# The remainders of weight units 6, 8, 10 and 12 made on GpSimd, in halves, in place of VectorE

## The chip, the cores and the metric

The kernel runs on one core of one Trainium2 chip. The metric is the device time of one execution in microseconds (us), the median of several runs. The engines are TensorE (PE, matrix products), VectorE (DVE), ScalarE (ACT), GpSimd (POOL), and SyncE (SP), which here only issues DMAs. Each engine works through its own list of instructions in order, and waits on semaphores for the others.

## The reference

A decoder trunk of two layers on 512 tokens of width 1024, in float32. Each layer normalises its input, multiplies it by one wide input projection, mixes tokens (layer 0: retention in chunks; layer 1: a causal convolution of 31 taps), adds a cross-attention over 256 memory tokens, gates the result, multiplies by an output projection, normalises, and adds to the residual:

```python
def reference(x, mem, ...):
    mem_kv = rmsnorm(mem, mem_norm_g) @ w_mem_kv
    mem_k, mem_v = jnp.split(mem_kv, 2, axis=-1)
    for i in range(DEPTH):                       # DEPTH = 2
        h = rmsnorm(x, norm_pre_g[i])
        branch, xq, gate = ...                   # from h @ w_in
        xa = memory_attention(xq, mem_k, mem_v)
        y = jnp.concatenate([branch, xa], axis=-1) * jax.nn.silu(gate)
        x = x + rmsnorm(y @ w_out, norm_post_g[i])
    return x
```

What matters here is the very beginning: the memory's projection into keys and values, and the first columns of layer 0's input projection.

## The kernel before

**Weights come in units.** All weight matrices are cut into units of 256 rows by 512 columns (a tile of 128 partitions x 2 x 512 float32, 512 KB), numbered in the order of use. Units 0 to 3 are the memory's keys, 4 to 7 its values, 8 to 11 the first 512 columns of layer 0's projection, 12 to 15 the next 512, and so on.

**Each float32 product is three matmuls.** A weight unit is split into a rounded part `whi` (ScalarE, line 192) and a remainder `wlo = wraw - whi` (VectorE, line 196, one instruction over 128 x 1024; or GpSimd, line 199, two instructions over 128 x 512, one for each half k of the unit). The activations are split in the same way (line 471 on ScalarE, line 475 on VectorE). `split3` (lines 302 to 304) then multiplies high by high, high by low and low by high. In this text hi9 is the rounded part of unit 9 and lo9 its remainder.

**Which engine makes a remainder** is decided by the unit's number in `conv_units`. Before the change, units 1 to 13 are VectorE's; from unit 14 to 55 GpSimd makes them in halves.

**Buffers set the order of the loads.** Three raw buffers (`wraw`) take turns: the load of unit i+3 (SP's list, line 172) waits until both parts of unit i have been made from the raw data. SP issues in order, so a load that waits holds the ones behind it. There are five buffers each of `whi` and `wlo`.

**Around units 6 to 14** the lists also hold: the sum of squares of the memory and of the two token halves of x. For each, ScalarE squares (line 484, two instructions), GpSimd adds the two results (line 485), VectorE reduces them (line 489), and TensorE adds over partitions by small matmuls (line 498); VectorE copies that out (line 500) and GpSimd makes the reciprocal root (lines 382 and 385). The second reciprocal root, of x, is needed to evacuate the first projection (line 870) and starts the table of rotary angles on VectorE (lines 390 and 804 on), which ScalarE's sine (line 840) waits for.

**Units 8 to 11 are used twice** (`proj_halves`): first for tokens 0 to 255, units 8 and 9 and then 10 and 11, and again for tokens 256 to 511. Their buffers come free only after the second use, so hi13 and hi14 wait for TensorE.

The whole order is written out by hand (a manual schedule): an instruction stands in its engine's list where the program calls it.

Of the kernel before, what the change touches and what calls it, by code (L numbers as in the profile page):

```python
# [46 lines left out]
LATE = 123  # L47
# [47 lines left out]
def trunk(ctx, tc, x, x_t, mem_t, pos, g_cols, w_mem, post_g, w0, w1, dw_w, dw_b,  # L95
# [11 lines left out]
    def nm(s):  # L107
        uid[0] += 1
        return f"{s}_{uid[0]}"
# [53 lines left out]
    def send(upto):  # L163

        for i in range(sent["dma"], min(upto, sent["conv"] + 3, nu)):
            sent["dma"] = i + 1
            if i in PRE:
                continue
            raws[i] = gp.tile([P, 2, G], F32, tag="wraw", bufs=3, name=nm("wraw"))
            src = units[i].rearrange("p (k c) -> p k c", k=2)  # L170
            for ks in (slice(0, 1), slice(1, 2)) if i == 0 else (slice(0, 2),):
                nc.sync.dma_start(out=raws[i][:, ks], in_=src[:, ks])

    def conv_units(upto):
        for i in range(sent["conv"], min(upto, nu)):
            send(i + 1)
            hi = gp.tile([P, 2, G], F32R, tag="whi", bufs=5, name=nm("whi"))
            lo = gp.tile([P, 2, G], F32R, tag="wlo", bufs=5, name=nm("wlo"))
            his[i], los[i] = hi, lo
            sent["conv"] = i + 1  # L180
            if i in PRE:
                nc.sync.dma_start(out=hi.bitcast(F32), in_=ahead[i][:, :, 1])
                nc.sync.dma_start(out=lo.bitcast(F32), in_=ahead[i][:, :, 0])
                continue
            raw = raws.pop(i)
            if i == 0:
                for k in range(2):
                    nc.scalar.copy(out=hi[:, k], in_=raw[:, k])
                    nc.vector.tensor_tensor(out=lo[:, k], in0=raw[:, k], in1=hi[:, k].bitcast(F32),
                                            op=ALU.subtract)  # L190
            else:
                nc.scalar.copy(out=hi, in_=raw)  # L192
            if i == 0:
                pass
            elif i < 14 or 56 <= i < 72 or i in (73, 74, 75) or i > LATE:
                nc.vector.tensor_tensor(out=lo, in0=raw, in1=hi.bitcast(F32), op=ALU.subtract)  # L196
            else:
                for k in range(2):
                    nc.gpsimd.tensor_tensor(out=lo[:, k], in0=raw[:, k],  # L199
                                            in1=hi[:, k].bitcast(F32), op=ALU.subtract)  # L200
# [40 lines left out]
    def prefetch():  # L241

        n = sent["use"]
        base = min(held) if held else n - 1
        conv_units(min(n + sent["ahead"], base + 5))
        send(sent["conv"] + 3)

    def next_unit(hold=False):
        i = sent["use"]
        sent["use"] += 1  # L250
        if hold:
            held.append(i)
        conv_units(i + 1)
        prefetch()
        return his.pop(i), los.pop(i)
# [263 lines left out]
    def evac_v(a, acc):  # L519
        nc.scalar.activation(out=mv[:, a, :], in_=acc, func=AF.Copy, scale=mr["c"][:, a:a + 1])  # L520

    conv = lambda upto: lambda: (conv_units(upto), send(upto + 3))
    mT = lambda kp: lambda: split_c(mt, kp, gcols[:, 0], mget)
    mT(0)()
# [973 lines left out]
```

## Time and profile before

| | us |
|---|---|
| median of 3 runs | 816.2 (816.07 to 820.01) |
| the profiled execution | 818.56 |
| its span, first to last instruction | 816.6 |
| PE busy in the span | 800.4 (98%) |
| DVE busy | 493.2 (60%) |
| ACT busy | 372.5 (46%) |
| POOL busy | 456.7 (56%) |

The span is that of one profiled execution. PE is busy nearly all the time, so what the time can lose or gain is in the few places where it stands idle, and in the chains that end in one of them. Rows give start, duration, engine, line, operation, the tiles, and in square brackets the engine's idle time before it and what ended that. An xN row is N instructions that followed each other, with their time together.

### The profile page before, as it was taken

The numbers are of one execution on the slowest core, as the hardware profiler recorded it, in microseconds if no ns is written. First come the engines' busy times: TensorE is split into PE (matmuls) and PEld (weight loads), VectorE is DVE, ScalarE is ACT, GpSimd is POOL, SyncE is SP. The second block draws the span as 40 slices with busy tenths as digits, with TensorE's granted clock in tenths as the row PEclk, the third lists the DMA queues.
The fourth block names the chain that finished last, engine by engine and source line by source line (L and its number), as shares of the span: only waits on it lengthen the run. The fifth ranks groups of instructions, "written<-read, shape, count | busy, mean of one in ns | idle before, by whom it ended". The sixth has DMA issues, their size and how long they took to land.

```text
span 816.6 us, 10729 instructions
## 1 busy us (share of the span) xinstructions
PE 800.4 (98%) x3910; PEld 675.4 (83%) x3910; DVE 493.2 (60%) x776; ACT 372.5 (46%) x625; POOL 456.7 (56%) x407
## 2 busy tenths in 40 slices
PE   8999999999999999999999999999999989899996
PEld 8888788888888888888888988888888878778885
DVE  5789212125655732353325579999999899656723
ACT  6752467622311233453425415545368786355511
POOL 1144754368777876411133036999775898867202
PEclk9999999999999999999999999999999999989999
DMA  7732764464364274676873364334543601323422
GB/s 265 258 106 96 243 205 137 155 206 164 132 207 163 95 218 146 210 238 212 271 243 124 130 230 149 132 130 161 179 147 98 215 31 52 127 80 104 166 92 103
DMA packets 47077, 131.14 MB, mean 161 GB/s; under 512 B 5297, under 2 KB 6961, under 8 KB 46769
## 3 DMA queue, kind: packets, MB, share of 16 engines
q1 hardware_dynamic: 46448, 130.25, 47.1%
q8 instruction: 30, 0.49, 0.3%
q10 hardware_dynamic: 576, 0.21, 0.1%
q14 instruction: 23, 0.18, 0.1%
HBM read 103.18 MB, written 27.26 MB: 160 GB/s over the span
## 4 chain that ended last, share of the span: by engine, by line
PE 74%; DVE 11%; ACT 6%; issue 3%; DMA 3%; POOL 3%; POOLq 0%; SPq 0%; DVEq 0%; ACTq 0%
PE mm L302 21%; PE mm L304 21%; PE mm L303 21%; DVE acc L1184 5%; PE tp L602 2%; DMA wraw<-in_w_mem 1%; DVE cy L1393 1%; POOL wlo L199 1%; PE acc L990 1%; ACT whi L192 1%; DVE wlo L196 1%; PE tp L971 1%; PE acc L992 1%; ACT cy L1387 1%; PE tp L948 1%
## 5 line engine op out<-in xcount | busy, mean ns | idle before, releaser
L302 PE MATMUL mm<-big,whi 128*128 128x512 f32 (+1 forms) x608 | 235.3, 387 | 1.7 <-ACT big L639 1.0
L304 PE MATMUL mm<-big,wlo 128*128 128x512 f32 (+1 forms) x608 | 228.0, 375 | 1.3 <-DVE wlo L196 1.0
L199 POOL TENSOR_TENSOR wlo<-wraw,whi 128x512 fp32r<-128x512 f32 x138 | 180.0, 1328 | 86.6 <-ACT whi L192 86.5
L303 PE MATMUL mm<-big,whi 128*128 128x512 f32 (+1 forms) x608 | 227.5, 374 | 0.0
L1184 DVE SCALAR_TENSOR_TENSOR acc<-gl,taps,acc 128x512 f32<-128x512 f32 x259 | 173.2, 746 | 0.1
L304 PE MATMUL mm<-whi,big 128*128 128x512 f32 (+1 forms) x432 | 167.1, 387 | 0.2 <-POOL big L767 0.2
L302 PE MATMUL mm<-whi,big 128*128 128x512 f32 (+1 forms) x408 | 162.4, 398 | 0.0
L303 PE MATMUL mm<-wlo,big 128*128 128x512 f32 (+1 forms) x408 | 157.8, 387 | 0.3 <-DVE wlo L196 0.3
L304 PEld LDWEIGHTS mm<-big,wlo 128*128 128x128 f32 x608 | 115.0, 189 | 23.0 <-DVE wlo L196 1.4
L302 PEld LDWEIGHTS mm<-big,whi 128*128 128x128 f32 x608 | 115.1, 189 | 21.4 <-ACT big L639 1.4
L303 PEld LDWEIGHTS mm<-big,whi 128*128 128x128 f32 x608 | 115.2, 189 | 18.8 <-issue 0.5
L192 ACT CAST whi<-wraw 128x1024 fp32r<-128x1024 f32 x111 | 115.5, 1047 | 24.5 <-PE mm L304 10.4
L1140 POOL TENSOR_TENSOR part<-part,pr 128x512 f32<-128x512 f32 x79 | 101.4, 1312 | 24.9 <-ACT pr L1139 24.7
L229 POOL TENSOR_TENSOR stage<-stage 128x512 f32<-128x512 f32 x44 | 57.2, 1301 | 103.6 <-ACT stage L228 99.8
L304 PEld LDWEIGHTS mm<-whi,big 128*128 128x128 f32 x432 | 81.1, 188 | 17.5 <-POOL big L767 0.6
L303 PEld LDWEIGHTS mm<-wlo,big 128*128 128x128 f32 x408 | 76.8, 188 | 15.5 <-DVE wlo L196 0.8
L302 PEld LDWEIGHTS mm<-whi,big 128*128 128x128 f32 x408 | 76.7, 188 | 14.7 <-issue 0.2
L196 DVE TENSOR_TENSOR wlo<-wraw,whi 128x1024 fp32r<-128x1024 f32 x42 | 56.3, 1349 | 43.0 <-ACT whi L192 43.0
L228 ACT CAST stage<-stage 128x512 fp32r<-128x512 f32 x44 | 27.3, 620 | 95.6 <-DMA stage<-in_w 53.4
L1139 ACT ACTIVATE pr<-gl,taps 128x512 f32<-128x512 f32 x79 | 53.6, 719 | 7.4 <-POOL part L1140 7.4
L1111 ACT ACTIVATE gl<-mm 128x512 f32<-128x512 f32 x12 | 7.2, 599 | 47.7 <-PE mm L304 47.7
L560 DVE TENSOR_REDUCE tiny<-tp 128x2 f32<-128x512 f32 x16 | 10.7, 687 | 25.7 <-PE tp L553 25.7
(221 smaller groups left out, 906.5 us busy)
## 6 DMA issues: line engine op xcount, KB each, us to landing
wraw<-in_w SPq DMA_DIRECT2D x104, 512.0 KB, 4.2
ahead<-stage SPq DMA_DIRECT2D x44, 512.0 KB, 5.2
stage<-in_w SPq DMA_DIRECT2D x44, 256.0 KB, 5.3
whi<-ahead SPq DMA_DIRECT2D x22, 512.0 KB, 4.2
wlo<-ahead SPq DMA_DIRECT2D x22, 512.0 KB, 5.9
wraw<-in_w_mem SPq DMA_DIRECT2D x7, 512.0 KB, 5.0
big<-in_x_t SPq DMA_DIRECT2D x2, 1024.0 KB, 7.3
o<-in_x SPq DMA_DIRECT2D x1, 2048.0 KB, 9.8
```

Source lines behind the costliest of these rows:

```text
L192: nc.scalar.copy(out=hi, in_=raw)
L196: nc.vector.tensor_tensor(out=lo, in0=raw, in1=hi.bitcast(F32), op=ALU.subtract)
L199: nc.gpsimd.tensor_tensor(out=lo[:, k], in0=raw[:, k], in1=hi[:, k].bitcast(F32), op=ALU.subtract)
L228: nc.scalar.copy(out=st[:, 1].bitcast(F32R), in_=st[:, 0])
L229: nc.gpsimd.tensor_tensor(out=st[:, 0], in0=st[:, 0], in1=st[:, 1], op=ALU.subtract)
L302: nc.tensor.matmul(dst, lh, rh, start=start, stop=False)
L303: nc.tensor.matmul(dst, lh, rl, start=False, stop=False)
L304: nc.tensor.matmul(dst, ll, rh, start=False, stop=stop)
L602: nc.tensor.matmul(po[:, h * P:(h + 1) * P], mv[:, m, h * P:(h + 1) * P], pT[:, m, h, :], start=m == 0, stop=m == 1)
L1139: nc.scalar.activation(out=pr, in_=gl[:, k:k + S], func=AF.Copy, scale=tap)
L1140: nc.gpsimd.tensor_tensor(out=parts[ct], in0=parts[ct], in1=pr, op=ALU.add)
L1184: nc.vector.scalar_tensor_tensor(out=o, in0=gl[:, k:k + S], scalar=tap, in1=ac, op0=ALU.mult, op1=ALU.add)
```

## The change

One condition gets an exception: for units 6, 8, 10 and 12 the first branch no longer holds, so they fall to the last branch, which makes the remainder on GpSimd in two halves. Units 7, 9, 11 and 13 stay on VectorE.

```diff
             if i == 0:
                 pass
-            elif i < 14 or 56 <= i < 72 or i in (73, 74, 75) or i > LATE:
+            elif i < 14 and i not in (6, 8, 10, 12) or 56 <= i < 72 or i in (73, 74, 75) or i > LATE:
                 nc.vector.tensor_tensor(out=lo, in0=raw, in1=hi.bitcast(F32), op=ALU.subtract)
             else:
                 for k in range(2):
                     nc.gpsimd.tensor_tensor(out=lo[:, k], in0=raw[:, k],
                                             in1=hi[:, k].bitcast(F32), op=ALU.subtract)
```

GpSimd's list before, from the sum of the memory's squares (first row) to the first remainder that it makes, that of unit 14 (last two rows). The rows of line 485 are the sums of squares of the memory and of the two halves of x; lines 382 and 385 the memory's reciprocal root.

```order
10 L485 TENSOR_TENSOR w_26_236<-w_26_236,w_27_237 128x1024 [waits Activation_49]
11 L382 TENSOR_SCALAR tiny_341<-tiny_337 128x2 [waits DVE_49]
12 L385 TENSOR_TENSOR tiny_343<-tiny_341,nhalf 128x2 [waits Pool_49]
13 L485 TENSOR_TENSOR w_60_413<-w_60_413,w_61_414 128x1024 [waits Activation_49]
14 L485 TENSOR_TENSOR w_73_473<-w_73_473,w_74_474 128x1024 [waits Activation_49]
15 L199 TENSOR_TENSOR wlo_546<-wraw_433,whi_545 128x512 [waits DMAHW0_49,Activation_49]
16 L199 TENSOR_TENSOR wlo_546<-wraw_433,whi_545 128x512
```

The same stretch of GpSimd's list after; wlo_313, 357, 403 and 445 are lo6, lo8, lo10 and lo12.

```order
11 L199 TENSOR_TENSOR wlo_313<-wraw_228,whi_312 128x512 [waits DMAHW7_49,PE_49,Activation_49]
12 L199 TENSOR_TENSOR wlo_313<-wraw_228,whi_312 128x512
13 L382 TENSOR_SCALAR tiny_342<-tiny_338 128x2 [waits DVE_49]
14 L385 TENSOR_TENSOR tiny_344<-tiny_342,nhalf 128x2 [waits Pool_49]
15 L199 TENSOR_TENSOR wlo_357<-wraw_283,whi_356 128x512 [waits DMAHW1_49,PE_49,Activation_49]
16 L199 TENSOR_TENSOR wlo_357<-wraw_283,whi_356 128x512
17 L199 TENSOR_TENSOR wlo_403<-wraw_335,whi_402 128x512 [waits DMAHW3_49,PE_49,Activation_49]
18 L199 TENSOR_TENSOR wlo_403<-wraw_335,whi_402 128x512
19 L485 TENSOR_TENSOR w_60_416<-w_60_416,w_61_417 128x1024 [waits Activation_49]
20 L199 TENSOR_TENSOR wlo_445<-wraw_385,whi_444 128x512 [waits DMAHW6_49,PE_49,Activation_49]
21 L199 TENSOR_TENSOR wlo_445<-wraw_385,whi_444 128x512
22 L485 TENSOR_TENSOR w_73_477<-w_73_477,w_74_478 128x1024 [waits Activation_49]
```

Eight instructions are new. The pairs of units 6 to 10 stand ahead of the first sum of x's squares, the pair of unit 12 between the two.

VectorE's list after, from the reduction of the memory's squares (first row) to the remainder of unit 13 (last row); wlo_332, 382, 433 and 538 are lo7, lo9, lo11 and lo13.

```order
10 L489 TENSOR_REDUCE w_27_237<-w_26_236 128x256
11 L196 TENSOR_TENSOR wlo_332<-wraw_263,whi_331 128x1024
12 L500 COPY tiny_338<-tp_337 128x2
13 L475 SCALAR_TENSOR_TENSOR big_301<-big_204,gcols,big_300 128x256 x4
14 L196 TENSOR_TENSOR wlo_382<-wraw_317,whi_381 128x1024
15 L475 SCALAR_TENSOR_TENSOR big_303<-big_204,gcols,big_302 128x256 x4
16 L196 TENSOR_TENSOR wlo_433<-wraw_361,whi_432 128x1024
17 L475 SCALAR_TENSOR_TENSOR big_301<-big_373,gcols,big_300 128x256 x4
18 L489 TENSOR_REDUCE w_61_417<-w_60_416 128x256
19 L475 SCALAR_TENSOR_TENSOR big_303<-big_373,gcols,big_302 128x256 x2
20 L489 TENSOR_REDUCE w_74_478<-w_73_477 128x256
21 L475 SCALAR_TENSOR_TENSOR big_303<-big_373,gcols,big_302 128x256 x2
22 L196 TENSOR_TENSOR wlo_538<-wraw_407,whi_537 128x1024
```

Before, one more remainder stood ahead of lo7 (lo6), between the four instructions of line 475 (lo8), behind the first row of big_303 (lo10), and behind lo11 (lo12). The rest is in the same order.

On SP the difference of the two lists shows the loads of units 8 (wraw_283) to 11; the wait behind each load is for the unit three before it.

```order
 L172 DMA wraw_283<-in_w 128x1024 [waits DMAHW5_49,DVE_49]
-L172 DMA wraw_316<-in_w 128x1024 [waits DMAHW7_49,DMAHW2_49,DVE_49]
-L172 DMA wraw_334<-in_w 128x1024 [waits DMAHW0_49,DVE_49]
-L172 DMA wraw_359<-in_w 128x1024 [waits DMAHW1_49,DVE_49]
-L459 DMA big_371<-in_x_t 128x2048
...
+L172 DMA wraw_317<-in_w 128x1024 [waits DMAHW2_49,DMAHW7_49,Activation_49,Pool_49]
+L172 DMA wraw_335<-in_w 128x1024 [waits DMAHW0_49,DVE_49]
+L172 DMA wraw_361<-in_w 128x1024 [waits DMAHW1_49,Activation_49,Pool_49]
+L459 DMA big_373<-in_x_t 128x2048
```

The loads stand in the same order. Those of units 9 and 11 wait for GpSimd where they waited for VectorE, and the load of x's second half (big_373) stands behind the one of unit 11.

## Rows read from the trace of the kernel before

**Rows 1.** The page: busy time of each engine, share, instructions.
```profile
PE 800.4 (98%) x3910; PEld 675.4 (83%) x3910; DVE 493.2 (60%) x776; ACT 372.5 (46%) x625; POOL 456.7 (56%) x407
```

**Rows 2.** Timeline of TensorE: start, us, line, tiles, [idle before <- releaser].
```profile
27.52 0.39 PE L303 MATMUL mm<-wlo,big 128*128 128x512 f32 x1
...
39.58 0.50 PE L303 MATMUL mm<-wlo,big 128*128 128x512 f32 x1 [0.34 <-DVE wlo L196]
...
49.05 0.95 PE L498 MATMUL tp<-ones,w 128*128 128x1 f32 x8
...
83.81 0.50 PE L302 MATMUL mm<-big,whi 128*128 128x512 f32 x1 [1.01 <-ACT big L639]
```

**Rows 3.** Timeline of VectorE and GpSimd where both make remainders, and GpSimd alone.
```profile
300.59 2.53 POOL L199 TENSOR_TENSOR wlo<-wraw,whi 128x512 fp32r<-128x512 f32 x2
...
333.73 3.53 POOL L199 TENSOR_TENSOR wlo<-wraw,whi 128x512 fp32r<-128x512 f32 x2
...
334.38 1.72 DVE L196 TENSOR_TENSOR wlo<-wraw,whi 128x1024 fp32r<-128x1024 f32 x1 [2.21 <-ACT whi L192]
```

**Rows 4.** Timeline of GpSimd, 36 to 55 us.
```profile
36.05 2.39 POOL L485 TENSOR_TENSOR w<-w,w 128x1024 f32<-128x1024 f32 x1 [7.45 <-ACT w L484]
43.30 2.41 POOL L485 TENSOR_TENSOR w<-w,w 128x1024 f32<-128x1024 f32 x1 [4.86 <-ACT w L484]
50.37 2.55 POOL L199 TENSOR_TENSOR wlo<-wraw,whi 128x512 fp32r<-128x512 f32 x2 [4.66 <-ACT whi L192]
...
53.28 1.03 POOL L385 TENSOR_TENSOR tiny<-tiny,nhalf 128x4 f32<-128x4 f32 x1
```

**Rows 5.** Timeline of ScalarE, 23 to 75 us: the casts of units 6, 9, 10, 11, 12, 14 among others.
```profile
23.59 1.05 ACT L192 CAST whi<-wraw 128x1024 fp32r<-128x1024 f32 x1 [2.16 <-DMA wraw<-in_w_mem]
...
29.32 1.05 ACT L192 CAST whi<-wraw 128x1024 fp32r<-128x1024 f32 x1 [0.86 <-PE mm L303]
...
32.46 1.04 ACT L192 CAST whi<-wraw 128x1024 fp32r<-128x1024 f32 x1
...
35.87 1.04 ACT L192 CAST whi<-wraw 128x1024 fp32r<-128x1024 f32 x1
38.67 1.05 ACT L192 CAST whi<-wraw 128x1024 fp32r<-128x1024 f32 x1 [1.75 <-DMA wraw<-in_w]
...
41.23 1.99 ACT L484 ACTIVATE w<-big 128x1024 f32<-128x1024 f32 x2
...
49.25 1.05 ACT L192 CAST whi<-wraw 128x1024 fp32r<-128x1024 f32 x1 [0.30 <-PE mm L304]
...
74.20 0.42 ACT L840 ACTIVATE q<-q 128x256 f32<-128x256 f32 x1 [11.70 <-DVE q L794]
```

**Rows 6.** Timeline of VectorE, 25 to 51 us.
```profile
25.94 1.22 DVE L196 TENSOR_TENSOR wlo<-wraw,whi 128x1024 fp32r<-128x1024 f32 x1
...
36.95 2.58 DVE L196 TENSOR_TENSOR wlo<-wraw,whi 128x1024 fp32r<-128x1024 f32 x1 [2.19 <-ACT whi L192]
...
40.90 1.67 DVE L475 SCALAR_TENSOR_TENSOR big<-big,gcols,big 128x256 fp32r<-128x256 f32 x4
42.48 2.05 DVE L489 TENSOR_REDUCE w<-w 128x256 f32<-128x1024 f32 x1
...
46.32 2.01 DVE L489 TENSOR_REDUCE w<-w 128x256 f32<-128x1024 f32 x1
...
49.04 1.21 DVE L196 TENSOR_TENSOR wlo<-wraw,whi 128x1024 fp32r<-128x1024 f32 x1
```

**Rows 7.** The chain that ended last, and SP's timeline: the loads of units 9 and 12.
```profile
25.93 3.30 DMA wraw<-in_w
...
31.66 0.33 SPq L172 DMA_DIRECT2D wraw<-in_w  x1
```

**Rows 8.** Late wait of TensorE, and the stretch around it: PE busy (count), granted clock, DMA.
```profile
711.20 0.35 PE L1356 MATMUL tp<-ones,sum 128*128 128x1 f32 x2 [2.59 <-DVE sum L1348]
...
710.00:720.00 10.00, 8.80 (x33) 0.66 0.37 139
```

## The prediction, made before the changed kernel ran

> **What bounds the kernel now.** I read the page first. TensorE is busy 98% of the span [rows 1], so work that is only moved from one helper engine to another cannot show unless it ends or starts a wait of TensorE. The idle times of TensorE came next: up to 100 us they are small, and between 20 and 80 us there is a single one, 0.34 us at 39.58, ended by VectorE's lo11; the next is 1.01 us at 83.81, ended by ScalarE [rows 2]. All the moved instructions run before 45 us. So the most that a relieved VectorE can give back here is 0.34 us and perhaps a part of the 1.01; whatever the change delays in front of TensorE is lost for good, since behind it TensorE is full.
>
> Then I read the three helpers. ScalarE makes hi9 at 29.32 as soon as its load has landed, and the chain that ended last runs through it: load of unit 9 (25.93 to 29.23), hi9, ScalarE's other work, hi11 (ends 36.91), lo11 [rows 5 to 7]. So the early part is a load chain whose first link is the end of lo6. Last I looked at how VectorE and GpSimd get in each other's way. A pair of halves takes 2.53 us alone, 1.27 each; the pair at 333.73 took 3.53, and the remainder that VectorE began in its midst took 1.72 in place of 1.22 [rows 3, 6]. They did not overlap: VectorE waited for the end of the first half, ran, and the second half waited for VectorE. Likewise lo11 began at 36.95, the sum of squares on GpSimd ended at 38.44, and lo11 ended 1.09 us behind that [rows 4, 6]. So an instruction that subtracts or adds two tiles on VectorE and one on GpSimd exclude each other, and where both have work they take turns.
>
> The Trainium skill, "Perfetto Trace Analysis", section "Optimizing Scalar/DVE Operations", speaks against the change: VectorE and GpSimd share a read port, so moving operations between those two might not help. By that rule the time freed on VectorE, 4 x 1.22 us, is worth nothing, which is a sum of zero or worse; by reading the two engines as independent the change would come out as the port rival below does. The pair of 3.53 us sides with the rule.
>
> **The change part by part.** Removed: four VectorE instructions of 1.22 us [rows 6]. Added: eight GpSimd halves, 10.1 us [rows 3]. GpSimd has room for them, so the cost is not their sum but where each stands. A remainder now takes 2.53 us, or 3.53 with a turn of VectorE, in place of 1.22: it is 1.3 to 2.3 us later. Who waits for that:
>
> *Unit 6.* hi6 ends at 24.64 [rows 5]; GpSimd starts 0.07 later, as it does behind hi14 (50.30, 50.37) [rows 4, 5], so the first half runs from 24.71 to 25.98. VectorE asks for lo7 at 25.94 [rows 6], 0.04 before that. If it gets its turn (case A), the second half ends at 24.71 + 3.53 = 28.24; if GpSimd goes on first (case B), at 27.24. TensorE wants the second half at 27.52 [rows 2]: A costs 0.77 us and about 0.1 of restart, B nothing.
>
> *The load of unit 9* waits for the end of lo6, and holds the loads behind it on SP. It goes at 28.27 (A) or 27.27 (B) in place of 25.93: +2.34 or +1.34. The load's own 3.30 us [rows 7] stays; hi9 and all that ScalarE does behind it, up to hi11, move by as much, since ScalarE has practically no idle time there.
>
> *lo11.* hi10 ends at 33.50 + 2.34 = 35.84; its pair runs to 38.44; the sum of squares, itself moved to 38.39, starts then and ends at 40.83. lo11 is locked out as before and ends 1.09 later, 41.92; TensorE goes on at 41.97 in place of 39.58 [rows 2, 4, 6]. TensorE is then 2.4 us late in A (unit 6's loss is inside that), 1.4 in B. The halves of units 8 and 10 themselves arrive in time.
>
> *Unit 12 and the second sum.* Unit 12's load waits for lo9, so in A it goes at 34.0 in place of 31.66 and hi12 ends at 42.06 in place of 39.72 [rows 5, 7]. lo12 itself is not wanted for a long time; its pair is harmful as a neighbour. Before, four instructions of line 475 (0.42 each) ran undisturbed at 40.90, and the first reduction at 42.48 lay beside GpSimd's second sum [rows 4, 6]. Now the pair (from 42.13) takes turns with those four: first half to 43.40, one instruction, second half to 45.0, two instructions to 45.8. The second sum asks at 43.30 + 2.34 = 45.64, before the fourth, and takes its 2.4 us, to 48.15. Then follow the fourth (48.55), the first reduction (2.05, to 50.6), two of line 475 (51.4) and the second reduction (2.01, to 53.4). TensorE wants that in the second half of its eight small matmuls, 49.45 before [rows 2] and 51.85 now: it waits 1.5 us, and is about 3.9 late. In B by the same steps the reduction ends at 53.0, and TensorE is 3.6 late.
>
> *Unit 14 and the root.* lo13 was done when GpSimd began unit 14's pair at 50.37 [rows 4, 6]. Now hi14, tied to TensorE, ends at 52.7, and the pair shares its time with two of line 475, pushing lo13 to 57.2; the reciprocal root (53.28 to 54.31 before) ends near 58.5, +4.2 (A), or 57.7, +3.4 (B). The rotary table on VectorE starts behind it; ScalarE waits for that at 74.20 for 11.70 us [rows 5], and TensorE's wait at 83.81 hangs on ScalarE. The slip of the root therefore replaces TensorE's own slip there: the 1.01 us idle would swallow a part of TensorE's slip only if the root slipped less.
>
> Sum: +4.2 in A, +3.4 in B. Nothing behind 84 us is changed. I take +3.7, between the two and nearer to neither, as the request of lo7 and the end of the half are 0.04 us apart. The profiled execution, 818.56 (816.6 of span and 1.96 around it), would become 822.3; the median shown is 2.36 below that execution, so the forecast is 816.2 + 3.7 = 819.9 us. That is 0.45% and so just inside what a measurement of this kernel can tell from no change, 0.5% or 4.1 us.
>
> **The rivals.**
>
> *The second collision does not happen.* If the fourth instruction of line 475 asks before the second sum (0.16 us apart above), the first reduction lies beside the sum as before, the second ends near 51.3, and TensorE does not wait. Then the slip is 2.4 to 2.8 in A, 1.4 in B: 817.6 to 819.0. For it: so small a distance. Against it: both times hang on hi12, so that a late load does not change their order.
>
> *The port is no obstacle between these instructions.* Then lo6 ends at 27.24, lo11 runs beside the sum of squares and ends at 39.3, before it did, and both reductions are in time: -0.2, 816.0 us; with part of the 1.01 us at 83.81 it could be 815.3. Against it stand the 3.53 and the 2.58 us [rows 3, 6].
>
> *The loads take longer.* Units 9 and 10 now go out almost together, and unit 11 and x's second half later and closer to unit 12. If unit 9 takes 4.5 us in place of 3.3, each later step slips by 1.2 more: 821.1.
>
> *The clock falls: clearly slower.* Behind the wait of 2.59 us at 711.20, with small matmuls around it, the granted clock was 0.66 over 10 us [rows 8]: the lower level, 1.2 GHz, for some 6.8 us, at a price of 0.34 x 10 = 3.4 us. If the wait for lo11 (2.4 us less what unit 6 has taken) or the one for the reduction does the same, the time is 819.9 + 3.4 = 823.3. [...] The Trainium skill, "TensorE: Matmul & The Clock Gate", section "Part 1: The HAM clock gate", has the same direction: an idle array falls back to the lower level.
>
> **How the numbers follow.** The forecast, with its two cases from 3.4 to 4.2, has 0.5; its own range with an uncertainty of 0.8 for the turns is 818.8 to 821.2. No second collision 0.22; longer loads 0.11; the clock 0.07; no obstacle 0.10. The range for 8 in 10 leaves out the lowest of the last and the highest of the clock: 816.5 to 823.0. Slower by over 0.5% (above 820.3): a third of the forecast's share, 0.17, the longer loads and the clock, 0.18, and about 0.02 of the rest: 0.37. Faster by over 0.5%: only what no row explains, 0.03. Within: 0.60.
>
> **What would show it.** In the changed kernel's timeline: the pair of unit 6 at 3.5 us (A) or 2.5 (B), with TensorE idle near 27.6 in A alone; the load of unit 9 issued at 27.3 or 28.3; the wait for lo11 near 41 with 1 us or more; VectorE's second reduction ending near 53 and TensorE idle before the small matmuls; the root of x ending near 58. The prediction is wrong if TensorE has no wait at the second reduction, or if lo7 and lo11 run at 1.22 us beside GpSimd's work, or if the slip at 84 us is not that of the root.

## The result, and the profile after

The changed kernel takes 822.28 us (median of 15 runs, 816.88 to 825.89), the kernel before, run alternately on the same chip, 816.14 (15 runs, 815.02 to 821.32). The ratio is 1.0054 with a 95% interval of 1.0036 to 1.0072: slower by 4.4 us, 2.9 to 5.9. (The ratio weighs all runs; the two medians alone are 6.1 apart.) Forecast were 819.9, between 816.5 and 823.0: the time is in the range, near its upper end, and the change is just beyond the 0.5% that the prediction called the limit of telling it from none. The profiled execution took 823.97, with a span of 822.2, against 818.56 and 816.6 before: +5.4 in time, +5.6 in the span.

The page after, first part; its columns are those of [rows 1].

```profile
PE 802.4 (98%) x3910; PEld 676.5 (82%) x3910; DVE 494.5 (60%) x772; ACT 372.4 (45%) x625; POOL 470.4 (57%) x415
```

VectorE has four instructions fewer, GpSimd eight more, as intended. Yet VectorE is no less busy, 494.5 us against 493.2: the four remainders saved are gone again in longer instructions. The timeline of TensorE after, its rows with a wait:

```profile
28.71 0.50 PE L303 MATMUL mm<-wlo,big 128*128 128x512 f32 x1 [1.17 <-POOL wlo L199]
...
42.40 0.50 PE L303 MATMUL mm<-wlo,big 128*128 128x512 f32 x1 [1.81 <-DVE wlo L196]
...
52.88 0.58 PE L498 MATMUL tp<-ones,w 128*128 128x1 f32 x4 [0.56 <-DVE w L489]
59.23 0.50 PE L302 MATMUL mm<-big,whi 128*128 128x512 f32 x1 [0.17 <-ACT vb L870]
...
87.87 0.50 PE L302 MATMUL mm<-big,whi 128*128 128x512 f32 x1 [1.14 <-ACT big L639]
...
662.99 2.24 PE L602 MATMUL tp<-w,mv 128*128 128x128 f32 x11 [2.34 <-ACT w L596]
...
716.84 0.35 PE L1356 MATMUL tp<-ones,sum 128*128 128x1 f32 x2 [2.62 <-DVE sum L1348]
```

Where [rows 2] had one wait of 0.34 us between 20 and 80 us, there are four now: for the second half of lo6, for lo11, for the second reduction, and a small one for the first evacuation behind the root. The wait of 0.34 at 39.58 has become 1.81 at 42.40, 2.82 later; the one at 83.81 stands at 87.87, 4.06 later. The next two rows belong to the late part of the program, to which the text returns below.

GpSimd after, with its idle times:

```profile
25.09 3.57 POOL L199 TENSOR_TENSOR wlo<-wraw,whi 128x512 fp32r<-128x512 f32 x2 [6.12 <-ACT whi L192]
...
38.87 2.39 POOL L485 TENSOR_TENSOR w<-w,w 128x1024 f32<-128x1024 f32 x1
41.22 3.72 POOL L199 TENSOR_TENSOR wlo<-wraw,whi 128x512 fp32r<-128x512 f32 x2
44.90 2.58 POOL L485 TENSOR_TENSOR w<-w,w 128x1024 f32<-128x1024 f32 x1
53.15 3.91 POOL L199 TENSOR_TENSOR wlo<-wraw,whi 128x512 fp32r<-128x512 f32 x2 [5.67 <-ACT whi L192]
...
57.42 1.03 POOL L385 TENSOR_TENSOR tiny<-tiny,nhalf 128x4 f32<-128x4 f32 x1
```

These are the pair of unit 6, the first sum of x's squares, the pair of unit 12, the second sum, the pair of unit 14, and the root. VectorE after, in the same stretch:

```profile
26.31 1.23 DVE L196 TENSOR_TENSOR wlo<-wraw,whi 128x1024 fp32r<-128x1024 f32 x1 [1.87 <-ACT whi L192]
...
39.79 2.55 DVE L196 TENSOR_TENSOR wlo<-wraw,whi 128x1024 fp32r<-128x1024 f32 x1 [3.78 <-ACT whi L192]
42.27 5.88 DVE L475 SCALAR_TENSOR_TENSOR big<-big,gcols,big 128x256 fp32r<-128x256 f32 x4
48.07 1.97 DVE L489 TENSOR_REDUCE w<-w 128x256 f32<-128x1024 f32 x1
...
50.75 1.99 DVE L489 TENSOR_REDUCE w<-w 128x256 f32<-128x1024 f32 x1
...
53.44 1.21 DVE L196 TENSOR_TENSOR wlo<-wraw,whi 128x1024 fp32r<-128x1024 f32 x1
```

Read the two side by side. lo7 (26.31 to 27.54) lies inside the pair of unit 6, which takes 3.57 us where a pair alone takes 2.53 [rows 3]: VectorE had its turn between the halves. lo11 asks at 39.79, in the midst of GpSimd's sum (38.87 to 41.26), and takes 2.55: it ends 1.08 behind the sum. The four instructions of line 475, 1.67 us together before [rows 6], take 5.88 between the pair of unit 12 and the second sum, and push both reductions.

ScalarE's cast of unit 9, and the chain that ended last, after (of the chain: start, duration, engine or DMA, tile):

```profile
32.12 1.05 ACT L192 CAST whi<-wraw 128x1024 fp32r<-128x1024 f32 x1 [3.28 <-DMA wraw<-in_w]
```

```profile
25.09 3.57 POOL wlo L199 x2
28.69 3.33 DMA wraw<-in_w
```

The load of unit 9 goes when GpSimd's second half ends, 2.76 later than in [rows 7], and hi9 follows 2.80 later.

Late in the program the windows after show one thing more (busy time and count of PE, PEld, DVE, ACT, POOL, then the granted clock, DMA share, GB/s):

```profile
660.00:664.00 4.00, 1.66 (x10) 1.20 (x9) 4.00 (x8) 3.97 (x7) 3.92 (x4) 0.94 0.00 0
664.00:668.00 4.00, 4.00 (x18) 3.64 (x18) 3.00 (x6) 2.72 (x7) 3.31 (x3) 0.63 0.00 0
```

Behind the wait of 2.34 us at 662.99 the granted clock falls to 0.63 over 4 us, part of that at the lower level, 1.2 GHz. In the execution of before the row that answers reads as follows, and the clock stays at 1.00 from 656 to 672 us (second row, a window).

```profile
658.92 2.05 PE L602 MATMUL tp<-w,mv 128*128 128x128 f32 x16 [2.29 <-ACT w L596]
656.00:672.00 16.00, 13.71 (x81) 11.64 (x80) 15.30 (x25) 14.24 (x25) 14.72 (x12) 1.00 0.10 34
```

There TensorE was 662.99 - 658.92 = 4.07 late; at 716.84 it is 716.84 - 711.20 = 5.64 late [rows 8]. So of the +5.6 in the span, some 4.1 were lost before 88 us, and 1.6 between the two places, where the clock fell.

### The profile page after: what moved, and what is told of

Read it like the earlier page. It is cut to its first block, busy times and chain, and to the rows that moved or that the text cites. A ratio compares the mean times of both kernels' runs of the same rounds, so it can differ in the third digit from the quotient of the medians.

```text
span 822.2 us, 10737 instructions
## 1 busy us (share of the span) xinstructions
PE 802.4 (98%) x3910; PEld 676.5 (82%) x3910; DVE 494.5 (60%) x772; ACT 372.4 (45%) x625; POOL 470.4 (57%) x415
## 4 chain that ended last, share of the span: by engine, by line
PE 69%; DVE 13%; ACT 6%; issue 4%; POOL 3%; DMA 3%; SPq 0%; POOLq 0%; DVEq 0%; ACTq 0%
PE mm L302 19%; PE mm L304 19%; PE mm L303 19%; DVE acc L1184 5%; DMA wraw<-in_w_mem 2%; POOL wlo L199 2%; PE tp L602 1%; DVE cy L1393 1%; PE acc L990 1%; DVE cy L1262 1%; ACT whi L192 1%; PE tp L971 1%; PE acc L992 1%; ACT cy L1387 1%; PE tp L948 1%
## 5 line engine op out<-in xcount | busy, mean ns | idle before, releaser
L199 POOL TENSOR_TENSOR wlo<-wraw,whi 128x512 fp32r<-128x512 f32 x146 | 193.6, 1349 | 100.3 <-ACT whi L192 100.2
L196 DVE TENSOR_TENSOR wlo<-wraw,whi 128x1024 fp32r<-128x1024 f32 x38 | 51.4, 1361 | 47.9 <-ACT whi L192 47.9
```

The source lines that it names most:

```text
L199: nc.gpsimd.tensor_tensor(out=lo[:, k], in0=raw[:, k], in1=hi[:, k].bitcast(F32), op=ALU.subtract)
```

## The experiments

Every run is timed against the kernel before on the same chip. One caution for all of them: the load of unit 6 itself, which no edit touches, lands at another time in each profiled execution (hi6 starts at 23.59 in that of before, at 23.96 after, between 22.86 and 25.00 in all), and what hangs on it moves along. Slips are therefore counted from the start of hi6. For the changed kernel at the wait near 84 us: (87.87 - 23.96) - (83.81 - 23.59) = 3.69 us. The kernel before, profiled a second time, shows +0.33 by the same count, so smaller differences are not read. Each kernel has one profiled execution.

| run | ratio, 95% interval | slip at lo11 | wait for 2nd reduction | slip of the root's end | slip near 84 us |
|---|---|---|---|---|---|
| the changed kernel | 1.0054 (1.0036 to 1.0072) | 2.45 | 0.56 | 3.77 | 3.69 |
| only6 | 1.0053 (1.0028 to 1.0077) | 2.72 | none | 3.16 | 3.46 |
| u6_8_10 | 1.0063 (1.0035 to 1.0091) | 2.92 | none | 3.37 | 3.52 |
| u8_10_12 | 1.0011 (0.9989 to 1.0032) | 0.21 | none | 0.29 | 0.39 |
| whole6 | 1.0017 (0.9995 to 1.0040) | 1.23 | none | 1.29 | 1.60 |
| raw9_apart | 1.0026 (1.0009 to 1.0043) | 0.94 | 0.55 | 2.26 | 2.42 |
| u6_8_10_raw9 | 1.0011 (0.9992 to 1.0030) | 0.96 | none | 1.41 | 1.49 |
| whole6_raw9 | 1.0030 (1.0010 to 1.0050) | 0.77 | 0.54 | 2.12 | 2.26 |
| u8_raw9 | 1.0014 (0.9992 to 1.0035) | -0.03 | 0.56 | 1.31 | 1.41 |
| before_raw9_apart | 1.0009 (0.9992 to 1.0025) | -0.70 | none | -0.26 | -0.06 |
| after_u14_vector | 1.0052 (1.0030 to 1.0075) | 2.58 | 0.55 | 2.87 | 3.02 |
| before_u14_vector | 0.9995 (0.9976 to 1.0013) | 0.07 | none | -0.99 | 0.12 |

**Which unit: only6, u8_10_12, u6_8_10.** The condition names fewer units (the three added lines are those of the three kernels, in that order):

```diff
-            elif i < 14 and i not in (6, 8, 10, 12) or 56 <= i < 72 or i in (73, 74, 75) or i > LATE:
+            elif i < 14 and i not in (6,) or 56 <= i < 72 or i in (73, 74, 75) or i > LATE:
+            elif i < 14 and i not in (8, 10, 12) or 56 <= i < 72 or i in (73, 74, 75) or i > LATE:
+            elif i < 14 and i not in (6, 8, 10) or 56 <= i < 72 or i in (73, 74, 75) or i > LATE:
```

> Only unit 6 is moved to GpSimd; 8, 10 and 12 are back on VectorE. Load theory (the end of lo6 sets the load of unit 9 and by it hi9, hi11 and lo11): the load of unit 9 is about 2.5 us later than before, TensorE is 2.4 to 2.8 us late after lo11, does not wait for the second reduction, and is 2.7 to 3.6 us late at the wait before 88 us; most of the changed kernel's 4.06 us is there. Rival (each of the four pairs costs its own share): a quarter, 1.0 us.

> Units 8, 10 and 12 are on GpSimd, unit 6 is back on VectorE. Load theory: the load of unit 9 goes at its old time, TensorE is at most 0.3 us late after lo11; what is left is the collision of unit 12's pair with line 475 and the second sum, 0 to 1.7 us, so 0.3 to 2.0 us in all before 88 us. Rival (each pair costs its share): three quarters, 3.0 us.

> Units 6, 8 and 10 are on GpSimd, unit 12 is back on VectorE. Collision theory: TensorE is 2.8 us late after lo11 as in the changed kernel, but the wait of 0.56 us for the second reduction is gone, and before 88 us it is 2.8 to 3.6 us late. Rival (the wait for the reduction comes from the late loads alone, not from unit 12's pair): the 0.56 us stay and the slip is 4.0 us.

With unit 6 alone most of the slip is there; with the other three alone, nothing that can be measured. TensorE in only6:

```profile
28.64 0.50 PE L303 MATMUL mm<-wlo,big 128*128 128x512 f32 x1 [1.06 <-POOL wlo L199]
...
42.59 0.50 PE L303 MATMUL mm<-wlo,big 128*128 128x512 f32 x1 [2.05 <-DVE wlo L196]
...
52.02 0.95 PE L498 MATMUL tp<-ones,w 128*128 128x1 f32 x8
...
87.56 0.50 PE L302 MATMUL mm<-big,whi 128*128 128x512 f32 x1 [1.52 <-ACT big L639]
```

The wait for lo11 is there, the one for the second reduction is not. Taken by themselves these three runs seem to clear the pair of unit 12. The runs further down show that this would be the wrong reading. Part of it lies in unit 9's load, which took 3.63 us in only6's execution and 3.79 in u6_8_10's, against 3.33 in the changed kernel's, for no reason that the edits give: 0.3 and 0.5 us of their slips come from there.

**The turn inside the pair: whole6.** The changed kernel, with lo6 in one GpSimd instruction, so that VectorE finds no gap in it:

```diff
+            elif i == 6:
+                nc.gpsimd.tensor_tensor(out=lo, in0=raw, in1=hi.bitcast(F32), op=ALU.subtract)
             else:
                 for k in range(2):
```

> As the changed kernel, but the remainder of unit 6 is one GpSimd instruction over 128 x 1024, so that VectorE cannot take a turn in its midst. Turn theory: lo6 ends about 2.4 us after it starts (3.57 in the changed kernel), the load of unit 9 goes 1.1 us earlier than there, TensorE waits 0.2 us or less for unit 6, is 1.4 to 1.8 us late after lo11, and 2.9 to 3.4 us late before 88 us. Rival (the end of lo6 hangs on GpSimd's speed, not on the turn): no difference, 4.06 us.

GpSimd and VectorE in whole6:

```profile
25.47 2.39 POOL L198 TENSOR_TENSOR wlo<-wraw,whi 128x1024 fp32r<-128x1024 f32 x1 [6.07 <-ACT whi L192]
...
26.70 2.23 DVE L196 TENSOR_TENSOR wlo<-wraw,whi 128x1024 fp32r<-128x1024 f32 x1 [2.03 <-ACT whi L192]
```

Now lo7 is the one that waits (2.23 in place of 1.23), and lo6 is done 2.39 after its start in place of 3.57. The slip at lo11 falls from 2.45 to 1.23, by just the 1.2 us of VectorE's turn, and the time to 1.0017. In sizes the expectation was missed: TensorE still waits 0.57 us for unit 6 (0.2 or less expected), and near 84 us it is 1.60 late, where 2.9 to 3.4 were expected. The gain there is larger than the turn, since the collision of unit 12 costs TensorE no wait either in this kernel; why, is told below.

**The load of unit 9: raw9_apart, before_raw9_apart.** Unit 9's raw data gets a buffer of its own, so that its load need not wait for lo6; in the changed kernel, and in the kernel before. The loads behind it move up too: that of unit 10 now waits for lo6, of unit 11 for lo7, of unit 12 for lo8.

```diff
-            raws[i] = gp.tile([P, 2, G], F32, tag="wraw", bufs=3, name=nm("wraw"))
+            raws[i] = gp.tile([P, 2, G], F32, tag="w4" if i == 9 else "wraw",
+                              bufs=4 if i == 9 else 3, name=nm("wraw"))
```

> As the changed kernel, but the raw data of unit 9 has a buffer of another kind, so that its load does not wait for lo6; unit 10's load now stands behind lo6, unit 11's behind lo7. Load theory: hi9 starts near 28.5 us (32.12 in the changed kernel), TensorE still waits 0.8 to 1.2 us for unit 6's second half, but is only 0.9 to 1.3 us late at lo11 (2.82 there) and 1.0 to 2.0 us late before 88 us (4.06 there). Rival (VectorE's turns beside GpSimd's eight halves make the slip, loads or not): 3.5 us or more before 88 us.

> The kernel before, with unit 9's raw data in a buffer of its own, so that its load need not wait for lo6. If the load of unit 9 is the first link of the chain to lo11 in the kernel before too, TensorE's 0.34 us at 39.58 goes and little else changes, since the load waited only some 0.9 us there and the root of x still hangs on unit 14: ratio 0.999 to 1.000, the same within what can be measured. The rival, that the load was not on the path before: 0.34 us stay.

TensorE in raw9_apart:

```profile
28.67 0.50 PE L304 MATMUL mm<-wlo,big 128*128 128x512 f32 x1 [0.93 <-POOL wlo L200]
...
40.86 0.50 PE L304 MATMUL mm<-wlo,big 128*128 128x512 f32 x1 [0.32 <-DVE wlo L197]
...
51.34 0.58 PE L499 MATMUL tp<-ones,w 128*128 128x1 f32 x4 [0.55 <-DVE w L490]
...
86.57 0.50 PE L303 MATMUL mm<-big,whi 128*128 128x512 f32 x1 [1.39 <-ACT big L640]
```

lo6 is as late as before (the pair still takes 3.56), yet the wait for lo11 falls from 1.81 to 0.32: the loads behind lo6 were the link between the two. But near 84 us the slip is 2.42, between what was expected of the theory and of its rival: more than the late load was at work. In the kernel before, the load was a link too: lo11 comes 0.70 earlier, counted from hi6. But 0.23 us of TensorE's wait remain where none was expected, and near 84 us nothing is left of the gain.

**The second collision: whole6_raw9, u8_raw9, u6_8_10_raw9.** Combinations of the edits above: both edits in the changed kernel; the three units without unit 6, with the buffer apart; and raw9_apart with unit 12 back on VectorE.

> The changed kernel with both halves of the cause taken away: lo6 in one GpSimd instruction (so that lo7 gets no turn inside it) and unit 9's raw buffer apart. If late lo6 by VectorE's turn and the late load of unit 9 are the whole cause, TensorE loses 0.4 to 0.6 us at unit 6 and nothing more at lo11, and its slip before 88 us, counted from the cast of unit 6, is 0.3 to 0.9 us: ratio 1.000 to 1.001. If the pairs of units 8, 10 and 12 cost something of their own beside them, the slip is over 1.3 us.

> Units 8, 10 and 12 on GpSimd, unit 6 on VectorE, and unit 9's raw buffer apart: the version that could beat the kernel before, if VectorE's relief is worth something once the load of unit 9 is early. Then TensorE has no wait at 39.6 and the root of x comes earlier: ratio 0.998 to 0.9995. If the relief is worth nothing, since lo11 is locked out by GpSimd's sum of squares as before, the ratio is 1.000 to 1.002.

> The run with unit 9's raw buffer apart, once more, with the remainder of unit 12 back on VectorE. In that run TensorE's slip at the wait near 84 us, counted from the cast of unit 6, was 2.42 us: 0.94 of it at lo11, 1.48 behind it, where the pair of unit 12 stands between the instructions of line 475 and TensorE waits 0.55 us for the second reduction. If that second collision comes with the pair of unit 12, TensorE has no wait at the small matmuls of line 498, and the slip is 1.4 to 1.8 us; VectorE pays 1.2 us for lo12 itself. The rival, that the collision of line 475 with the second sum makes the same delay whether the pair stands between or not: slip 2.2 us or more. In time the two stand 0.6 to 1.0 us apart, near 1.0015 and 1.0026 as ratios.

whole6_raw9 was a miss: TensorE lost 0.18 us at unit 6 and 0.30 at lo11, and was still 2.26 late near 84 us. The first expectation of u8_raw9, that VectorE's relief would show once the load is early, failed as well: TensorE still waits 0.69 us for lo11, and 0.56 for the second reduction. Its other case, that the relief is worth nothing (1.000 to 1.002), fits the 1.0014.

```profile
39.86 0.50 PE L304 MATMUL mm<-wlo,big 128*128 128x512 f32 x1 [0.69 <-DVE wlo L197]
...
50.35 0.58 PE L499 MATMUL tp<-ones,w 128*128 128x1 f32 x4 [0.56 <-DVE w L490]
```

The table tells what is common. Between lo11 and 84 us the slip grows by 1.24 to 1.49 in the four kernels that have a wait for the second reduction as after does, with unit 12's pair among the instructions of line 475 (after 3.69 - 2.45, raw9_apart, whole6_raw9, u8_raw9). It grows by 0.05 to 0.74 in those without. after_u14_vector has that wait and that pair too, and grows by 0.44 only; it will show the way that the delay takes. u6_8_10_raw9 differs from raw9_apart in unit 12 alone, and was to decide. Its VectorE:

```profile
38.34 3.78 DVE L197 TENSOR_TENSOR wlo<-wraw,whi 128x1024 fp32r<-128x1024 f32 x2 [3.22 <-POOL wlo L200]
42.04 3.81 DVE L476 SCALAR_TENSOR_TENSOR big<-big,gcols,big 128x256 fp32r<-128x256 f32 x4
```

Line 475 (476 there) takes 3.81 with the second sum alone as its neighbour, against 5.88 with the pair as well; TensorE does not wait at the small matmuls, and the slip near 84 us is 1.49, as expected, in place of 2.42. So the pair of unit 12 costs 0.9 us there. The two times, 1.0011 and 1.0026, have intervals that overlap; it is the traces that tell them apart. They also show where the 0.9 us arise, unit 14's pair and lo13 in raw9_apart (first two rows) and in u6_8_10_raw9:

```profile
51.61 3.90 POOL L200 TENSOR_TENSOR wlo<-wraw,whi 128x512 fp32r<-128x512 f32 x2 [5.68 <-DVE big L476]
51.90 1.22 DVE L197 TENSOR_TENSOR wlo<-wraw,whi 128x1024 fp32r<-128x1024 f32 x1
...
51.79 3.03 POOL L200 TENSOR_TENSOR wlo<-wraw,whi 128x512 fp32r<-128x512 f32 x2 [6.22 <-ACT whi L193]
51.20 1.21 DVE L197 TENSOR_TENSOR wlo<-wraw,whi 128x1024 fp32r<-128x1024 f32 x1
```

Unit 14's pair starts 27.68 and 27.70 us behind hi6, at the same time. In raw9_apart VectorE is late by the collision, lo13 falls inside the pair and has its turn between the halves, as lo7 has in unit 6's; in u6_8_10_raw9 lo13 began before the pair. The pair is 0.87 us longer, and the root 2.26 - 1.41 = 0.85 later. It takes 3.90 to 3.92 us in all four kernels that grow by 1.24 or more, and 2.55 to 3.03 in the others; in after_u14_vector GpSimd does not make it. In the changed kernel, too, unit 14's pair starts 2.41 us later than before, as lo11 does (2.45), and the rest of the root's 3.77 is the pair's 3.91 in place of 2.55. So the pair of unit 12 costs its time by way of unit 14's pair and the root, and not by the wait for the second reduction.

In u8_10_12 the pair of unit 12 stands at the same place and hurts nothing:

```profile
41.22 2.73 POOL L199 TENSOR_TENSOR wlo<-wraw,whi 128x512 fp32r<-128x512 f32 x2 [1.16 <-ACT whi L192]
```

There hi12 waited for its load until 40.10, and the work of line 475 began only at 41.59, behind ScalarE's line 471. It still met the pair and took 3.43 us in place of 1.67; but the second sum came only at 44.73, with the fourth instruction of line 475 already begun, and did not lock it out. In whole6 it went the same way. ScalarE waited 1.78 us (u8_10_12) and 1.44 (whole6) for unit 12 behind hi11, and 0 to 0.88 in the five kernels that have the wait for the second reduction. So whether the collision reaches TensorE goes with how far unit 12 lands behind unit 11; no run changes this landing alone.

**What hangs on the root: after_u14_vector, before_u14_vector.** Unit 14's remainder, which stands ahead of the root in GpSimd's list, goes to VectorE, in either kernel (`i < 15` in place of `i < 14`).

> As the changed kernel, but the remainder of unit 14 is on VectorE, so that the reciprocal root of x stands behind no pair on GpSimd. Root theory (the slip at the wait before 88 us is that of the root): the root ends near 57.3 us in place of 58.45, TensorE is about 3.0 us late there in place of 4.06. Rival (TensorE's own lateness after the reductions, 3.46 us, sets it): 3.5 us or more.

> The kernel before with one edit: the remainder of unit 14 is on VectorE too. If the wait of 1.01 us at 83.81 us hangs on the root, the root ends near 53.0 us in place of 54.31, the wait goes, and the kernel is 1.0 us faster than before (0.12%, under what a comparison can tell, but to be seen in the trace). Rival (the wait hangs on ScalarE's or the loads' own pace): no change, 1.01 us stay.

In the changed kernel the slip fell by 0.67 us, from 3.69 to 3.02, as expected; the median did not show it. In the kernel before, the root came 0.99 earlier, and the wait near 84 us stayed (1.09 at 83.80): a miss. VectorE there shows why:

```profile
57.34 1.22 DVE L513 TENSOR_TENSOR mkT<-mkT,tp 128x1024 f32<-128x1024 f32 x1 [1.98 <-PE tp L396]
```

In before the same instruction stands at 57.43 with 0.96 of idle time. It waits for TensorE's small matmuls of line 396, and the rest of the rotary table is queued behind it: an earlier root makes it wait 1.0 longer, no more.

**The kernel before, once more: before_again.**

> The kernel before, profiled once more, with no edit: how much the start of hi6, lo11's wait and the waits at 84, 659 and 711 us differ between two executions of the same program. Expected: hi6 within 1.5 us of 23.59, the wait before lo11 and the one at 84 us as before to 0.2 us, and another clock at one of the late waits if these are chance.

```profile
39.70 0.50 PE L303 MATMUL mm<-wlo,big 128*128 128x512 f32 x1 [0.88 <-DVE wlo L196]
...
658.20 2.05 PE L602 MATMUL tp<-w,mv 128*128 128x128 f32 x16 [1.17 <-ACT w L596]
```

That the waits would be as before to 0.2 us was a miss: the one for lo11 was 0.88 in place of 0.34, since the load of unit 6 landed later against TensorE, the one near 84 us 1.33 in place of 1.01, and the one at 658 1.17 in place of 2.29. The same program differs by as much as some of the prediction's terms.

No version is shown to be faster than the kernel before; the lowest ratio, 0.9995 of before_u14_vector, is the same within its interval.

## Why the prediction was right, and where it was not

**That helpers could only lose** held. Nearly all loss up to 88 us is in waits of TensorE for the moved work and what it delays: its waits between 20 and 88 us add up to 4.85 us, 1.35 before. The pair of unit 6 took 3.56 to 3.59 us in six kernels, and lo6 in one piece 2.39 with a waiting lo7 of 2.23 in whole6. The Trainium skill, "SBUF — State Buffer", section "Who interferes with whom", says that an instruction of VectorE with two inputs in SBUF contends with one of GpSimd that reads it. These times agree with that.

***Unit 6*: the mechanism was right, its case was left open for no need.** Case A said 24.71 + 3.53; less the 0.37 us by which this execution's hi6 came later, 28.66 is 28.29. The pair took 3.56 to 3.59 wherever unit 6 was made in halves: VectorE's turn was no toss-up. The forecast of +3.7 lay halfway to case B, which no run showed. Case A by itself gave +4.2, 820.4 us; the slip of TensorE in the profiled execution is 4.06, or 3.69 from hi6. That 3.69 meets the 3.7 is luck: averaging with case B took off about as much as the steps of units 12 and 14, below, had added too much.

***The load of unit 9*** was right: 3.33 us against 3.30, and 1.5 us of slip at lo11 go when it no longer hangs on lo6 (raw9_apart: 0.94 for 2.45). ***lo11*** was right: TensorE at 41.97 forecast, 42.40 measured, 42.03 less the 0.37.

***Unit 12 and the second sum*: right in kind, too large in its wait.** The collision is there as described, pair, line 475 and second sum taking turns. The second reduction ends at 52.74, 52.37 less the 0.37 (53.4 forecast), and TensorE waits 0.56 in place of 1.5. The mis-sized term is unit 12's load: it went at 34.45 (34.0 forecast), but took 5.2 us where the sum kept the 6.9 of before. So hi12 was to end at 42.06, and ended at 40.84. What the step didn't see is what only6 shows: without the pair VectorE must make lo12 itself, and line 475 then meets the second sum. So part of the growth behind lo11 stays without the pair: 0.74 us in only6 and 0.60 in u6_8_10, against 1.24 in the changed kernel. The pair is thus worth some 0.5 to 0.6 us there, and 0.9 with unit 9's load out of the way; the slips of 3.52 (u6_8_10) and 3.69 (after) lie closer together only since unit 9's load was slower in u6_8_10's execution.

***Unit 14 and the root*: the number right, the reason only in part.** The root ended at 58.45, 58.08 less the 0.37, and 58.5 were forecast. Unit 14's pair shared its time with VectorE, but not as described: the two of line 475 were not held up (0.87 us at 52.66), and lo13, forecast to be pushed to 57.2, had its turn inside the pair and ended at 54.65. In the table the slip near 84 us follows that of the root within about 0.3 us in all kernels with a late one. But "TensorE's wait at 83.81 hangs on ScalarE" and so on the root is not the whole: before_u14_vector shows that line 513, tied to TensorE, holds the chain too. A later root moves the wait; an earlier one does not.

**"Nothing behind 84 us is changed" failed.** The rival of the clock looked at the waits for lo11 and the reduction, but there the clock did not fall: it is 1.00 from 28 to 90 us. It fell at 663 us in the profiled execution, for 1.6 us. Over all runs this can be weighed, as an estimate: a run's span times one less its mean granted clock is what the lower level took. That is some 4.1 us (standard error 0.5) in the changed kernel's 15 runs, 5.8 (0.5) in only6's ten, and 4.2 (0.2) in 29 of the kernel before on only6's chip. Span times clock, the rest, is 815.2 (0.4), 815.2 (0.3) and 812.2 (0.2). For the runs of the kernel before that alternated with the changed kernel the clock is not on record; on three chips its rest is 811.5 to 812.3. So +2.9 to +3.7 us are shown beyond the clock, and what more the median of 822.28 holds is not shown to be the change's doing.

In only6, u6_8_10 and after_u14_vector the lower level did take 1.4 to 1.7 us more than in the kernel before on the same chip; why it did not in the changed kernel's runs is open. Taken on each run's own chip, the rest grows by 3.0 us in only6 and after_u14_vector, 2.8 in u6_8_10, 2.3 in raw9_apart, 1.9 in whole6_raw9, 1.2 in whole6 and u6_8_10_raw9, 0.8 in u8_raw9, 0.1 in u8_10_12, 0.0 in before_raw9_apart, and by -0.4 in before_u14_vector (standard errors 0.3 to 0.6). These follow the table's last column, 0.0 to 0.7 us below it. Why some 3.0 remain of 3.7 at 84 us stays open: in the profiled execution nothing was given back, and the mean over runs may hold cases that it does not show.

**The other rivals.** *The port is no obstacle* fell with the pair of 3.57 us; *no second collision* fell with the wait of 0.56, though u8_10_12 shows that it can go that way; *longer loads* fell with the 3.33 (3.79 was the longest in the kernels whose load of unit 9 waits for lo6).

## What to carry to other kernels

Before a remainder, or any producer, is moved to an engine that is idle, ask what its end releases: here a late lo6 held back a buffer, so a load, and all that the load feeds, and the pair of unit 6 alone cost most of what all four did. Delays that stand one behind the other don't add and can't be acquitted one at a time: the pair of unit 12 cost TensorE nothing in u8_10_12, some 0.5 us in the changed kernel, and 0.9 with the load of unit 9 out of the way. Splitting an instruction in two also makes a gap in which the engine that competes for the same access gets in.

## What the runs showed of the hardware

- Two GpSimd halves of 128x512, issued back to back, let a waiting VectorE instruction of two tiles in between: 3.56 to 3.59 us for the pair, 1.23 for VectorE's. One instruction of 128x1024 took 2.39, and VectorE's waited and took 2.23. Unit 14's pair took 3.90 to 3.92 us where lo13 began inside it, 3.02 or 3.03 where lo13 had begun some 0.6 us before it (only6, u6_8_10, u6_8_10_raw9, before_raw9_apart), and 2.62 where lo13 was done (u8_10_12).
- Waits of nearly the same length were followed by either clock: at the same place of the program (line 602) the 16 matmuls behind waits of 2.29 (before) and 2.34 (u8_raw9) took 2.05 us at a granted clock of 1.00, those behind waits of 2.34 (after) and 2.33 (only6) 3.30 and 3.60, with 0.63 and 0.70 over 664 to 668 us. The wait itself was 1.15 to 1.17 in three other executions (before_again, before_raw9_apart, whole6_raw9).
- The landing of one load, unit 6's, moved by up to 2.1 us between the profiled executions (hi6 from 22.86 to 25.00), though no edit touches that load or what it waits for.
